# Rotary embedding, interleaved pairs: the first 2 MB loaded in fp32 pieces and stored early in fp32 over SyncE's queue, VectorE by 8 positions

## Chip, cores, metric

One core of a Trainium2 chip. The time is device microseconds of one execution; a profile's span is the part of it between the first and last instruction (316.0 us of a run that took 317.78). All times below are medians of fast runs unless a single profile is named.

## The reference

```python
# x: (8, 2048, 16, 64) fp32 ; cos, sin: (2048, 32) fp32
x1, x2 = x_pairs[..., 0], x_pairs[..., 1]
out1 = x1 * cos - x2 * sin
out2 = x1 * sin + x2 * cos          # out: pairs interleaved again, fp32
```

64 MiB go in, 64 MiB come out; there is little arithmetic per byte.

## The kernel before

A tile holds one batch in bf16: 128 partitions, each with 16 positions of 1024 elements. GpSimd's DMAs cast fp32 to bf16 on the way in and back on the way out; five tile buffers are in use. VectorE rotates in place with three instructions for each group of KP positions. Two things go over SyncE's queue, whose DMAs here do not cast: the first positions of batch 0 (fp32 into a staging buffer, ScalarE casts), and the last positions of batch 7 (ScalarE casts back).

```python
    KP = 4 ; NX = 5 ; HEAD = 2 ; TAIL = 4
    def store(b, k1=K):
        nc.gpsimd.dma_start(out=out_t[b, :, :k1], in_=tiles[b][:, :k1])
    def rotate(b, k0, k1):                     # three TENSOR_TENSOR on positions k0..k1
        ...
        head = stage.tile([P, TAIL, HD], fp32, name="st")
        for k in range(HEAD):
            nc.sync.dma_start(out=head[:, k : k + 1], in_=x_t[0, :, k : k + 1])
        nc.sync.dma_start(out=cos_sb, in_=cos_t)
        nc.sync.dma_start(out=sin_sb, in_=sin_t)
        load(0, HEAD)
        for b in range(1, NX):
            load(b)
        nc.scalar.copy(out=tiles[0][:, :HEAD], in_=head[:, :HEAD])
        # ... cos and sin spread into bf16 tables (VectorE)
        for b in range(B):
            # ... rotate(b, ...) over all positions
            if b < B - 1:
                store(b)
            if b >= 1 and b - 1 + NX < B:
                load(b - 1 + NX)               # waits until store(b - 1) has landed
        store(B - 1, K - TAIL)
        tail = stage.tile([P, TAIL, HD], fp32, name="st")
        nc.scalar.copy(out=tiles[B - 2][:1, 0, :1], in_=tiles[B - 1][:1, K - 1, :1])
        nc.scalar.copy(out=tail, in_=tiles[B - 1][:, K - TAIL :])
        nc.sync.dma_start(out=out_t[B - 1, :, K - TAIL :], in_=tail)
```

## Time and profile before

| | before |
|---|---|
| time, median of 6 runs | 317.45 us (317.34 to 317.79) |
| VectorE busy | 221.8 us (70%) |
| DMA queues' share of 16 engines | 96.8% + 3.1% |
| VectorE starts | 44.2 us |
| batch 1's store issued / its first row on a DMA engine | 102.2 / 120.6 us |

The two DMA queues' shares are to be read as one: together they are 99.9%, so the DMA engines are practically always full. The last row holds the slack: batch 1's store stood in the queue for 18 us before an engine got to it. The lines are in the prediction below.

### The profile page before, as it was taken

The numbers are of one execution on the slowest core, as the hardware profiler recorded it, in microseconds if no ns is written. First come the engines' busy times: TensorE is split into PE (matmuls) and PEld (weight loads), VectorE is DVE, ScalarE is ACT, GpSimd is POOL, SyncE is SP. The second block draws the span as 40 slices with busy tenths as digits, with TensorE's granted clock in tenths as the row PEclk, the third lists the DMA queues.
The fourth block names the chain that finished last, engine by engine and source line by source line (L and its number), as shares of the span: only waits on it lengthen the run. The fifth ranks groups of instructions, "written<-read, shape, count | busy, mean of one in ns | idle before, by whom it ended". The sixth has DMA issues, their size and how long they took to land.

```text
span 316.0 us, 198 instructions
## 1 busy us (share of the span) xinstructions
DVE 221.8 (70%) x102; ACT 6.9 (2%) x4; POOL 8.9 (3%) x20
## 2 busy tenths in 40 slices
DVE  0000039999999999999999999999999999100000
ACT  1200000000000000000000000000000000000400
POOL 3000000000000000000000000000000000000000
DMA  9899999999999999999999999999999999999996
GB/s 241 198 257 212 212 207 236 228 199 199 253 212 265 398 498 431 398 332 261 203 399 465 328 203 199 481 448 265 199 307 423 398 440 481 406 398 481 417 431 263
DMA packets 3025, 101.72 MB, mean 322 GB/s; under 512 B 336, under 2 KB 336, under 8 KB 848
## 3 DMA queue, kind: packets, MB, share of 16 engines
q0 software_dynamic: 2304, 98.04, 96.8%
q1 hardware_dynamic: 720, 3.67, 3.1%
q14 instruction: 1, 0.01, 0.0%
HBM read 67.63 MB, written 67.11 MB: 426 GB/s over the span
## 4 chain that ended last, share of the span: by engine, by line
another core or an unknown queue 91%; DMA 2%; ACTq 1%; ACT 1%; SPq 0%; issue 0%
DMA st<-in_x_dram 2%; ACTq L144 1%; ACT xt L92 1%; ACT L92 0%; SPq L85 0%; ACT xt L116 0%; ACTq L116 0%; ACTq L92 0%
## 5 line engine op out<-in xcount | busy, mean ns | idle before, releaser
L75 DVE TENSOR_TENSOR xt<-xt,c_tab 128x4096 bf16<-128x4096 bf16 (+1 forms) x33 | 73.5, 2228 | 1.1
L80 DVE TENSOR_TENSOR xt<-xt,qt 128x4096 bf16<-128x4096 bf16 (+1 forms) x33 | 73.5, 2228 | 1.1
L74 DVE TENSOR_TENSOR qt<-xt,s_tab 128x4096 bf16<-128x4096 bf16 (+1 forms) x33 | 73.5, 2228 | 1.1
L94 DVE CAST s_tab<-sin_sb 128x512 bf16<-128x512 f32 x1 | 0.5, 453 | 44.2 <-DMA sin_sb<-in_sin_dram 44.2
L59 POOL DMA_DIRECT2D out_dram<-xt x8 | 4.3, 535 | 202.1 <-DVE xt L80 202.1
L116 ACT COPY xt<-xt 1x1 bf16<-1x1 bf16 x1 | 0.2, 193 | 286.3 <-DMA out_dram<-xt 286.3
L56 POOL DMA_DIRECT2D xt<-in_x_dram x8 | 4.4, 561 | 52.1 <-DMA out_dram<-xt 51.3
L117 ACT CAST st<-xt 128x4096 f32<-128x4096 bf16 x1 | 3.6, 3599 | 0.0
L92 ACT CAST xt<-st 128x2048 bf16<-128x2048 f32 x1 | 1.9, 1899 | 0.0
L92 ACT ACT_TABLE_LOAD x1 | 1.3, 1283 | 6.4 <-DMA st<-in_x_dram 6.4
L96 DVE CAST c_tab<-cos_sb 128x1024 bf16<-128x1024 f32 x1 | 0.7, 684 | 0.0
L95 DVE TENSOR_SCALAR s_tab<-sin_sb 128x512 bf16<-128x512 f32 x1 | 0.4, 443 | 0.0
L133 POOL MEMSET const-float32-0.0<- 128x1 f32 x1 | 0.1, 99 | 0.2 <-issue 0.2
L133 POOL MEMSET const-bfloat16-1.0<- 128x1 bf16 x1 | 0.1, 102 | 0.0
L133 POOL MEMSET const-float32-1.0<- 128x1 f32 x1 | 0.1, 99 | 0.0
L133 POOL MEMSET const-uint8-127<- 128x1 uint8 x1 | 0.1, 99 | 0.0
## 6 DMA issues: line engine op xcount, KB each, us to landing
xt<-in_x_dram POOLq DMA_DIRECT2D x7, 4096.0 KB, 58.0
out_dram<-xt POOLq DMA_DIRECT2D x1, 6144.0 KB, 49.4
xt<-in_x_dram POOLq DMA_DIRECT2D x1, 3584.0 KB, 22.7
out_dram<-st SPq DMA_DIRECT2D x1, 2048.0 KB, 15.5
st<-in_x_dram SPq DMA_DIRECT2D x2, 512.0 KB, 4.5
cos_sb<-in_cos_dram SPq DMA_DIRECT2D x1, 256.0 KB, 22.4
sin_sb<-in_sin_dram SPq DMA_DIRECT2D x1, 256.0 KB, 42.1
out_dram<-xt POOLq DMA_DIRECT2D x7, 54.0
```

The source lines that it names most:

```text
L56: nc.gpsimd.dma_start(out=tiles[b][:, k0:], in_=x_t[b, :, k0:])
L59: nc.gpsimd.dma_start(out=out_t[b, :, :k1], in_=tiles[b][:, :k1])
L74: nc.vector.tensor_tensor(out=rows(qt[:, :nk]), in0=rows(xp), in1=tab(s_tab), op=mult)
L75: nc.vector.tensor_tensor(out=rows(xp), in0=rows(xp), in1=tab(c_tab), op=mult)
L80: nc.vector.tensor_tensor(out=x3, in0=x3, in1=q_swap, op=add)
L92: nc.scalar.copy(out=tiles[0][:, :HEAD], in_=head[:, :HEAD])
L94: nc.vector.tensor_copy(out=s2[:, :, 0], in_=sin_sb)
L95: nc.vector.tensor_scalar_mul(s2[:, :, 1], sin_sb, -1.0)
L96: nc.vector.tensor_copy(out=c_tab.rearrange("p k (i j) -> p (k i) j", j=2), in_=cos_sb.to_broadcast([P, K * D2, 2]),)
L117: nc.scalar.copy(out=tail, in_=tiles[B - 1][:, K - TAIL :])
L133: nc = _bacc.Bacc("TRN2", target_bir_lowering=False, num_devices=1)
L144: with _tile.TileContext(nc) as tc:
```

## The change

The intent: start on data that need no casting DMA, let the first part of the result leave while the loads still run, and spare VectorE some fixed costs.

```diff
-    KP = 4
+    KP = 8
-    HEAD = 2
+    HEAD = 4
+    HEAD_RUNS = [(0, 1), (1, 2), (2, 4)]
...
-    def store(b, k1=K):
-        nc.gpsimd.dma_start(out=out_t[b, :, :k1], in_=tiles[b][:, :k1])
+    def store(b, k0=0, k1=K):
+        nc.gpsimd.dma_start(out=out_t[b, :, k0:k1], in_=tiles[b][:, k0:k1])
...
-        head = stage.tile([P, TAIL, HD], fp32, name="st")
-        for k in range(HEAD):
-            nc.sync.dma_start(out=head[:, k : k + 1], in_=x_t[0, :, k : k + 1])
+        head = stage.tile([P, HEAD, HD], fp32, name="st")
+        for k0, k1 in HEAD_RUNS:
+            nc.sync.dma_start(out=head[:, k0:k1], in_=x_t[0, :, k0:k1])
...
                 rotate(b, 0, HEAD)
+                nc.scalar.copy(out=head, in_=tiles[b][:, :HEAD])
+                for k0, k1 in HEAD_RUNS:
+                    nc.sync.dma_start(out=out_t[b, :, k0:k1], in_=head[:, k0:k1])
                 rotate(b, HEAD, KP)
...
-                store(b)
+                store(b, HEAD if b == 0 else 0)
```

More of the change, by code (lines that the diff above doesn't have):

```diff
@@ L90 @@
             load(b)
-        nc.scalar.copy(out=tiles[0][:, :HEAD], in_=head[:, :HEAD])
+        nc.scalar.copy(out=tiles[0][:, :HEAD], in_=head)
         s2 = s_tab.rearrange("p k (i j) -> p (k i) j", j=2)
@@ L106 @@
             if b < B - 1:
-                store(b)
+                store(b, HEAD if b == 0 else 0)
             if b >= 1 and b - 1 + NX < B:
                 load(b - 1 + NX)
-        store(B - 1, K - TAIL)
+        store(B - 1, 0, K - TAIL)
         tail = stage.tile([P, TAIL, HD], fp32, name="st")
```

## The prediction

> **What bounds the kernel now.** The page of the kernel before comes first, its busy shares and slices, because they say which resource has no free time.
>
> ```profile
> DVE 221.8 (70%) x102; ACT 6.9 (2%) x4; POOL 8.9 (3%) x20
> DMA  9899999999999999999999999999999999999996
> GB/s 241 198 257 212 212 207 236 228 199 199 253 212 265 398 498 431 398 332 261 203 399 465 328 203 199 481 448 265 199 307 423 398 440 481 406 398 481 417 431 263
> q0 software_dynamic: 2304, 98.04, 96.8%
> q1 hardware_dynamic: 720, 3.67, 3.1%
> HBM read 67.63 MB, written 67.11 MB: 426 GB/s over the span
> ```
>
> VectorE is busy 70% of the span, the DMA engines practically always: every slice is an 8 or a 9 up to the last. The GB/s row seems to say that stores (about 420) run twice as fast as loads (about 210), but a load is counted by its bf16 bytes in SBUF and a store by its fp32 bytes in HBM. In HBM bytes both are the same. The whole traffic, 67.63 + 67.11 = 134.74 MB, went in 316.0 us, 426 GB/s with both ends of the span included.
>
> Next, the stretches of 5 us around the change from loads to stores:
>
> ```profile
> 90.00:95.00 5.00, 4.90 (x4) 0.00 (x0) 0.00 (x0) 1.00 0.97 210
> 95.00:100.00 5.00, 4.93 (x3) 0.00 (x0) 0.00 (x0) 1.00 1.04 210
> 100.00:105.00 5.00, 4.93 (x3) 0.00 (x0) 0.54 (x1) 1.00 0.98 419
> 105.00:110.00 5.00, 4.93 (x3) 0.00 (x0) 0.00 (x0) 1.00 0.98 419
> ```
>
> The two last columns are DMA share and GB/s: no dip where the five loads end and the first store begins. Then GpSimd's timeline, to see how far ahead of the DMA engines its queue is filled:
>
> ```profile
> 74.53 0.54 POOL L59 DMA_DIRECT2D out_dram<-xt  x1 [70.48 <-DVE xt L80]
> 102.17 0.54 POOL L59 DMA_DIRECT2D out_dram<-xt  x1 [27.11 <-DVE xt L80]
> 121.79 0.54 POOL L56 DMA_DIRECT2D xt<-in_x_dram  x1 [19.08 <-DMA out_dram<-xt]
> 130.09 0.53 POOL L59 DMA_DIRECT2D out_dram<-xt  x1 [7.77 <-DVE xt L80]
> ```
>
> The store of batch 0 is issued at 74.53 us, while by the trace's packet records the fifth load holds the DMA engines until 101; that is 27 us of slack. The store of batch 1 comes at 102.17, and the store of batch 0 lands at 121.79 (the load that waits for it starts then): 19 us of slack. This second slack is the smallest in the kernel, and the number to watch. Two landings that GpSimd waited for, 121.79 and 141.09, are one transfer of 8.39 MB apart: 19.3 us, or 435 GB/s.
>
> Last, what VectorE waited for at the start, and how long the table loads took:
>
> ```profile
> DVE s_tab L94 <- DMA sin_sb<-in_sin_dram: 44.2, 1, 44.2
> cos_sb<-in_cos_dram SPq DMA_DIRECT2D x1, 256.0 KB, 22.4
> sin_sb<-in_sin_dram SPq DMA_DIRECT2D x1, 256.0 KB, 42.1
> ```
>
> 256 KB would take 0.6 us at full rate. In the packet records each DMA engine has 8 rows of each table and 8 rows of each batch; one table row runs after each batch row (64 KB of fp32, 2.43 us). So cos takes as long as the load of batch 0, sin as long as that of batch 1. VectorE idles 44 us, but the DMA engines have loads to do until 101 us, so that costs nothing.
>
> **What the Trainium skill says.** "DMA: Bandwidth & Descriptors", section "Queues, rings and completion order": each DMA engine goes round robin over the queues that have work, a packet at a time. The trace agrees, with one row per turn: 22.4 and 42.1 us for the two tables. The same page, "Where 436 GB/s comes from", puts the ceiling of the fabric at 435 GB/s; the 19.3 us per 8.39 MB above are that. The same page's "Rules for kernel authors" says that spreading DMAs over issuing engines gains no bandwidth; before has both queues together at 99.9%, with a share near 1 whichever runs. "SBUF — State Buffer", section on the "DVE blocks DMA" trap, says that a VectorE instruction in a two-port mode keeps GpSimd from writing descriptors; with queues this full, no wait in this trace shows such a thing, and it bears on rival 2.
>
> **The change, part by part.**
>
> *Bytes.* 1 MB more of x comes, and 2 MB of the result goes, over SP as fp32 instead of over GpSimd with a cast. The HBM bytes stay 134.74 MB, and they set the DMA time. Shorter rows cost a little: 4 KB took 0.159 us where its share of a long row is 2.43/16 = 0.152. Over the two 4 KB pieces of the result (16 rows on each engine) that is 0.1 us; with the 8 KB rows and the shorter rows of batch 0, I allow 0.3 us.
>
> *Start.* The first two pieces are as before. By the packet records they hold all 16 engines from about 3 us until GpSimd's first rows start, at 5.1 to 6.0 us, so there is no hole for the third piece to fill. It stands in SP's order where cos stood, and should be served as cos was: one row after each row of batch 0.
>
> *VectorE's start.* The rows of batch 0's load are now 12 positions, 48 KB, 1.83 us; with one 8 KB row (0.3 us) each, 8 turns are 17 us: third piece in by about 23 us. Then cos beside batch 1, 8 x (2.42 + 0.08) = 20 us: 43. Then sin beside batch 2, 20 us: 63. VectorE starts at about 63.5 us, not 44.2.
>
> *VectorE's pace.* 2048 elements took 1.22 us and 4096 took 2.29, so 1.07 for each 2048 and about 0.16 fixed; 8192 should take 4.43, with the gap 4.47. A batch is then 6 x 4.47 = 26.8 us, before 12 x 2.33 = 28.0. From 63.5: tables 1.3, positions 0 to 3 in 3 x 2.33 = 7.0 (71.8), positions 4 to 7 another 7.0 (78.8), 8 to 15 in 3 x 4.47 = 13.4 (92.2). Batch 1 ends at 92.2 + 26.8 = 119.0. Tile buffers and loads don't hold it: the fifth load is in at about 102.
>
> *Early result.* ScalarE casts 128x4096 in 3.60 us as at the end of the kernel before, 71.8 to 75.5, and SP issues three pieces. Their 24 rows on each engine alternate with batch rows of about 2.4 us, so they would be in flight until some time beyond 115 us; nothing waits for them but the buffer of the tail, at 296 us.
>
> *The queue.* All work that the engines have before batch 1's store, from the first GpSimd row at 5.1 us: load of batch 0, 14.6; third piece 2.4; tables 1.3; four loads 77.4; store of batch 0 without its first 4 positions, 14.6; early result 4.8; in all 115.1 us. The same sum for before is 115.0, and predicts 120.1 where the records show batch 1's store starting at 120.6; so I add 0.5: the engines run dry at 120.7 (first engine) to about 121.6. Batch 0's store is issued at 92.2, ahead of 102: no hole. Batch 1's store is issued at 119.0. Its slack is 2 us where it was 19. How long GpSimd takes from issue to first packet is not bare in this trace: its first load, issued at 1.24, had its first row at 5.14, but behind SP's rows. With 1.5 to 2 us no engine idles, or for half a microsecond; with 3.9 us they idle 2 us. I put 0.5 us as the likely loss.
>
> *After that* slack grows again: batch 2's store comes at about 146 us, and by then the store of batch 1 and the sixth load (39 us of work) are queued. VectorE ends at about 281 us, not 269, but the last store only gets the engines at 294. The end (cast, tail over SP) is not changed.
>
> *Sum.* 317.4 + 0.3 (short rows) + 0.5 (hole at 121 us) = 318.2; with some chance of no loss at all, 318.1 us.
>
> **Rivals.** 1: mixing reads with writes early, or SP's path without a cast, moves more bytes per microsecond. For it: some slices read 498. Against it: these have a share above 1, because their packets are counted where they start, and whole transfers take 19.3 us whether loads or stores; and the SP rows ran no faster than the others. It would make 310 to 314 us. 2: the lost slack becomes a real hole, because VectorE starts later than I think, or because instructions of 4.4 us delay descriptors. Each microsecond beyond 2 is a microsecond of time; 5 us late makes 321. For it: a margin of 2 us out of a sum of 119 is thin. Against it: the SP rows still queued fill the first part of it, and that is already in the sum. 3: the third piece gets through before GpSimd's rows start, as the first two did. Then cos and sin land 20 us earlier, VectorE starts at 44, all slack stays, and the time is 317.4 to 317.7. Against it: cos, in the same place, did not get through. 4: VectorE by 8 positions as a gain. It saves 1.1 us per batch on an engine with idle time: nothing.
>
> **Range and chances.** DMA work cannot shrink, which closes the low end at 317.0. The high end is the hole: 2 us of it, and a little, 320.2. Faster by 2% would need 311 us, less than the bytes take at 435 GB/s (134.74 / 435 = 309.7) with the some 5 us of start and end: 1%. Slower by 2% needs 323.7, a hole of over 5 us: 4%.
>
> **What would show it.** VectorE's wait for sin ends near 63 us; the 8192-element instructions take 4.4 us; GpSimd issues the second store near 119; DMA shares stay near 1 with at most one dip, at 120 to 124 us. If VectorE starts at 44, rival 3 holds; if the DMA row shows several dips or a time above 321, the queue sum is wrong; a time below 316 would mean that the bytes do not set the DMA time.

## More of the kernel before

One more view belongs here, because it turned out to matter: what the trace keeps for the line on which the program ends. SyncE's entries there (number, then duration in ns, first and last start in us) and the issue of the tail's store, with 15.5 us to landing:

```profile
L144 SPq EVENT_SEMAPHORE  x9: 17/28/28, 300.0 to 315.9; - x9
L144 SPq DRAIN  x3: 7/7/7, 315.2 to 315.5; - x3
299.59 0.35 SPq L118 DMA_DIRECT2D out_dram<-st  x1
out_dram<-st SPq DMA_DIRECT2D x1, 2048.0 KB, 15.5
```

The tail (the last positions of batch 7) lands at 299.59 + 15.5 = 315.1 us, SyncE's first DRAIN, with which it ends its program, is at 315.2, and 0.8 us later the span ends.

## The result

| | before | after |
|---|---|---|
| time, median of 6 runs | 317.45 us | 318.18 us (318.07 to 318.25) |
| ratio, with 95% interval | | 1.0021 (1.0008 to 1.0034) |
| VectorE starts | 44.2 us | 63.5 us |
| batch 1's store issued / first row | 102.2 / 120.6 us | 119.2 / 120.6 us |

Ratios are the mean time of one kernel's fast runs over that of the other's of the same rounds, so not quite the ratio of the two medians. The time is the predicted one within 0.1 us, and the difference is small but outside the noise. The page, the waits and GpSimd's timeline of the changed kernel, to be laid beside those in the prediction:

```profile
DVE 214.2 (68%) x54; ACT 12.3 (4%) x5; POOL 8.9 (3%) x20
q0 software_dynamic: 2304, 95.42, 94.2%
q1 hardware_dynamic: 1296, 6.82, 6.3%
HBM read 67.63 MB, written 67.11 MB: 426 GB/s over the span
...
DVE s_tab L97 <- DMA sin_sb<-in_sin_dram: 63.5, 1, 63.5
...
92.42 0.54 POOL L62 DMA_DIRECT2D out_dram<-xt  x1 [88.38 <-DVE xt L83]
119.18 0.54 POOL L62 DMA_DIRECT2D out_dram<-xt  x1 [26.22 <-DVE xt L83]
120.39 0.53 POOL L59 DMA_DIRECT2D xt<-in_x_dram  x1 [0.67 <-DMA out_dram<-xt]
```

The HBM bytes are the same, some of them have gone from queue 0 to queue 1, and VectorE starts one load later. The slack has gone: GpSimd used to wait 19.08 us between the second store and the landing of the first one, and now waits 0.67. Whether that left the DMA engines idle is in the row for 118 to 124 us, cut into 40 slices. A packet is counted in the slice where it starts, so with long rows a full engine shows groups of 9 with zeros between; it is short rows that show a hole. First before, then after:

```profile
DMA  9999900000000000099999000000000099999000
```

```profile
DMA  0082888979797969699999900000000009999990
```

From 118.3 to 120.5 us the changed kernel's row is filled with small packets, SyncE's third piece of the early result; then batch 1's store starts. A count of the packets running at each moment shows 16, one on each engine, from 6 us to 311 us in both kernels. There is no hole.

So where are the 0.7 us? SyncE's entries on the program's last line, after:

```profile
L150 SPq EVENT_SEMAPHORE  x11: 17/28/28, 312.0 to 316.3; - x11
L150 SPq DRAIN  x3: 7/7/7, 315.5 to 315.8; - x3
299.60 0.33 SPq L124 DMA_DIRECT2D out_dram<-st  x1
out_dram<-st SPq DMA_DIRECT2D x1, 2048.0 KB, 15.4
```

The tail lands at 315.0 us, 0.1 us *earlier* than in the profile before, but the first DRAIN is at 315.5. The trace's records of single waits say why. At the end SyncE waits, one after another, on every semaphore that a DMA has used. In the records the 9 DMAs of its own queue use 8 semaphores in turn, so the ninth, the tail's store, shares that of the first load. In the list of waits that semaphore comes second; the 7 waits behind it, each long satisfied, start 61 ns apart and take 0.43 us. In the kernel before, the tail's store was the fifth of 5, and its wait was the last of the list. From last landing to end of span: 0.87 us before, 1.33 after. That is 0.45 of the 0.73 us between the medians.

The other 0.28 us, by subtraction, lie before the last landing, although the two profiles seem to say the opposite. The profile of the kernel before is of a run of 317.78 us, 0.33 above the median; the changed kernel's is of one of 318.12, 0.06 below its median. Two runs below, b_kp8 and a_noearly, take as long as the kernel before, and their profiles are of median runs: by the packet records batch 1's store has its first row at 120.30 and 120.34 us, and the tail lands at 314.92 and 314.90. Against these the changed kernel, with 120.56 and 315.03, is 0.2 us late at batch 1's store and 0.1 at the end.

### The profile page after: what moved, and what is told of

It reads as the page before. It is cut to its first block, busy times and chain, and to the rows that moved or that the text cites. A ratio compares the mean times of both kernels' runs of the same rounds, so it can differ in the third digit from the quotient of the medians.

```text
span 316.4 us, 162 instructions
## 1 busy us (share of the span) xinstructions
DVE 214.2 (68%) x54; ACT 12.3 (4%) x5; POOL 8.9 (3%) x20
## 4 chain that ended last, share of the span: by engine, by line
DVE 34%; issue 25%; another core or an unknown queue 20%; DMA 13%; ACT 1%; POOL 1%; ACTq 0%; POOLq 0%
DMA out_dram<-xt 13%; DVE xt L83 11%; DVE xt L78 11%; DVE qt L77 11%; ACT st L123 1%; POOL out_dram L62 1%; POOL xt L59 0%; DVE s_tab L97 0%; DVE s_tab L98 0%; POOLq L62 0%; DVE c_tab L99 0%; ACT xt L122 0%; ACTq L123 0%; ACTq L122 0%
## 5 line engine op out<-in xcount | busy, mean ns | idle before, releaser
L78 DVE TENSOR_TENSOR xt<-xt,c_tab 128x8192 bf16<-128x8192 bf16 (+1 forms) x17 | 71.0, 4175 | 0.6
L83 DVE TENSOR_TENSOR xt<-xt,qt 128x8192 bf16<-128x8192 bf16 (+1 forms) x17 | 71.0, 4175 | 0.6
L77 DVE TENSOR_TENSOR qt<-xt,s_tab 128x8192 bf16<-128x8192 bf16 (+1 forms) x17 | 71.0, 4174 | 0.5
L97 DVE CAST s_tab<-sin_sb 128x512 bf16<-128x512 f32 x1 | 0.5, 453 | 63.5 <-DMA sin_sb<-in_sin_dram 63.5
L106 ACT CAST st<-xt 128x4096 f32<-128x4096 bf16 x1 | 3.6, 3606 | 43.4 <-DVE xt L83 43.4
L123 ACT CAST st<-xt 128x4096 f32<-128x4096 bf16 x1 | 3.6, 3605 | 0.0
L95 ACT CAST xt<-st 128x4096 bf16<-128x4096 f32 x1 | 3.6, 3604 | 0.0
```

The costliest lines, as they stand in the source:

```text
L77: nc.vector.tensor_tensor(out=rows(qt[:, :nk]), in0=rows(xp), in1=tab(s_tab), op=mult)
L78: nc.vector.tensor_tensor(out=rows(xp), in0=rows(xp), in1=tab(c_tab), op=mult)
L83: nc.vector.tensor_tensor(out=x3, in0=x3, in1=q_swap, op=add)
L95: nc.scalar.copy(out=tiles[0][:, :HEAD], in_=head)
L97: nc.vector.tensor_copy(out=s2[:, :, 0], in_=sin_sb)
L106: nc.scalar.copy(out=head, in_=tiles[b][:, :HEAD])
```

## The experiments

The edits are against the changed kernel unless another is named. "Before" is the kernel before, run on the same chip in the same rounds. "End" is from the last landing to the end of the span, in the profile. Two theories stand: my sum (0.3 us for short rows, 0.5 for a hole), and the end waits. The runs were made on two chips; the kernel before took 317.48 to 317.51 us.

**a_again**: no edit.

> The changed kernel itself, as the reference of this call: 318.1 to 318.3 us, 0.6 to 0.8 us over the kernel before. Theory (end waits): the last DMA lands no later than in the kernel before, and about 0.4 us of the difference lie after that landing, in 7 further waits of SyncE of about 62 ns each. Rival (my sum): the last landing is 0.8 us later, and what follows it is the same.

Measured: 318.18 us, before 317.50, ratio 1.0023 (1.0009 to 1.0036). Last landing 315.01, end 1.33 us. As the first time. The last landing is 0.1 us later than in a_noearly and b_kp8, not 0.8, which speaks for the end waits.

**a_eight**: one DMA fewer.

```diff
-                for k0, k1 in HEAD_RUNS:
+                for k0, k1 in [(0, 2), (2, 4)]:
                     nc.sync.dma_start(out=out_t[b, :, k0:k1], ...
```

> The early result in 2 pieces of 8 KB rows in place of 3, so the kernel has 8 DMAs on SyncE's queue, not 9, and the tail's store does not share a semaphore with the first load. Theory (end waits): the wait for the tail becomes the last of SyncE's list, what follows the last landing drops from 1.3 to about 0.9 us, and the time by 0.4 us to about 317.8. Rival (rows and hole): the 4 KB rows gone save at most 0.1 us, time 318.1.

Measured: 317.88 us (317.66 to 317.95), ratio 1.0012 (0.9999 to 1.0025). SyncE's DRAIN and the tail's store:

```profile
L150 SPq DRAIN  x3: 7/7/7, 315.4 to 315.7; - x3
299.81 0.33 SPq L124 DMA_DIRECT2D out_dram<-st  x1
out_dram<-st SPq DMA_DIRECT2D x1, 2048.0 KB, 15.5
```

End 0.88 us: no wait between the tail's and the DRAIN. The list is as long as in the changed kernel (11 entries), so it is the tail's place in it that counts, not its length. The end moved as foreseen, by 0.45 us; the time by 0.30. The rest went into a later last landing (315.29 us, 0.26 later in this profile, which is of a run 0.07 above the median).

**b_nine**: four idle loads more in the kernel before.

```diff
         nc.sync.dma_start(out=sin_sb, in_=sin_t)
+        for i in range(4):
+            spare = consts.tile([P, 16], fp32, name=f"spare{i}")
+            nc.sync.dma_start(out=spare, in_=sin_t[:, i * 16 : (i + 1) * 16])
```

> The kernel before with 4 tiny loads more (64 bytes a row) on SyncE's queue, 9 in all; nothing reads them. Theory (end waits): the tail's store shares the first load's semaphore, its wait comes early in SyncE's list, and the time rises by 0.4 us to about 317.85 with no later last landing (32 rows of 64 bytes on each DMA engine are at most 0.1 us of DMA time). Rival: 317.4 to 317.5, unchanged.

Measured: 318.41 us (318.22 to 318.64), before 317.50, ratio 1.003 (1.0018 to 1.0043).

```profile
L147 SPq DRAIN  x3: 7/7/7, 316.1 to 316.4; - x3
300.00 0.35 SPq L121 DMA_DIRECT2D out_dram<-st  x1
out_dram<-st SPq DMA_DIRECT2D x1, 2048.0 KB, 15.6
```

End 1.31 us, not 0.87: the other direction of the same effect. The last landing also came 0.4 us later than in the kernel before, where I had foreseen 0.1. My 0.1 was too low: of the 512 small rows 384 are recorded with 24 ns, 64 with 51 and 64 with 2455 (about the time of one long row). At 24 ns, the 32 rows of an engine are some 0.8 us, an estimate from these records; that is enough for the 0.4, but which part of a record holds up other rows isn't shown.

**a_kp4**: VectorE by 4 positions, everything else as changed.

```diff
-    KP = 8
+    KP = 4
...
-                rotate(b, HEAD, KP)
-            for k0 in range(KP if b == 0 else 0, K, KP):
+                rotate(b, HEAD, 8)
+            for k0 in range(8 if b == 0 else 0, K, KP):
```

> The changed kernel with VectorE by 4 positions as before. VectorE then takes 28.0 us for a batch in place of 26.75: batch 1's store should be issued at about 120.9 us and not at 119.2, its first rows come 1.5 us later at 122.4, and the DMA engines run dry at 120.5 to 121.2. Theory (the slack at batch 1's store is used up): a hole of about 1.3 us opens, time 319.4 to 319.6. Rival (VectorE is hidden, as it is busy 68%): 318.2, as the changed kernel.

Measured: 319.34 us (319.19 to 319.39), ratio 1.0058 (1.0045 to 1.007), 1.16 us over the changed kernel and just under the foreseen 319.4. GpSimd's timeline and the DMA row of the same 118 to 124 us:

```profile
120.96 0.54 POOL L62 DMA_DIRECT2D out_dram<-xt  x1 [27.38 <-DVE xt L83]
DMA  0027498999999999945210000009900000000000
```

Now the small packets thin out (4, 5, 2, 1) at 120.6 to 121.1 us and zeros follow, until batch 1's store begins, everywhere at once, at 122.06. The packet records give 1.22 us idle on the mean engine. The store was issued 1.78 us later than in the changed kernel and cost 1.2, so the changed kernel had some 0.6 us of slack left, not 2. And with no row ahead of it, the delay from issue to first row is bare: 122.06 - 120.96 = 1.10 us.

**b_kp8**: the kernel before with KP = 8 alone.

> The kernel before with VectorE by 8 positions alone. VectorE's busy time falls by some 7 us to about 214.5 (fewer fixed costs of 0.16 us), none of it on the path of the DMA engines: 317.3 to 317.6, as the kernel before. Rival (coarser steps delay the first store, or long instructions delay GpSimd's descriptors): over 318.

Measured: 317.56 us (317.35 to 317.99), before 317.51, ratio 1.0004 (0.999 to 1.0018). VectorE is busy 214.2 us, 7.6 less, for nothing. In this kernel the part is worthless, and in the changed one it keeps 1.2 us away (a_kp4).

**a_four**: one SyncE piece more ahead of the tables.

```diff
-        for k0, k1 in HEAD_RUNS:
+        for k0, k1 in [(0, 1), (1, 2), (2, 3), (3, 4)]:
             nc.sync.dma_start(out=head[:, k0:k1], in_=x_t[0, :, k0:k1])
```

> The first 2 MB of x in four pieces of 4 KB rows in place of 4, 4 and 8 KB: one more piece ahead of the tables on SyncE's queue. If each piece takes as long as one batch's load (one row per turn), sin lands at about 82.9 us and not at 63.5. Theory (slack of 2 us): batch 0's store is issued at 112 and batch 1's at 138.5; the DMA engines have nothing to do for about 18 us in two holes, time about 336. Rival (a VectorE start some us later is hidden): under 320.

Measured: 337.30 us (337.15 to 337.48), ratio 1.0624 (1.061 to 1.0639). Waits, and stretches of 10 us with the DMA share in the last but one column:

```profile
83.36 0.45 DVE L97 CAST s_tab<-sin_sb 128x512 bf16<-128x512 f32 x1 [83.36 <-DMA sin_sb<-in_sin_dram]
...
100.00:110.00 10.00, 9.93 (x3) 0.00 (x0) 0.00 (x0) 1.00 0.49 205
110.00:120.00 10.00, 9.93 (x3) 0.00 (x0) 0.54 (x1) 1.00 0.74 315
120.00:130.00 10.00, 9.90 (x4) 0.00 (x0) 0.00 (x0) 1.00 0.74 315
130.00:140.00 10.00, 9.93 (x3) 0.00 (x0) 1.01 (x2) 1.00 0.00 0
```

VectorE starts 19.8 us later than in the changed kernel, and two holes open, 7.0 us before batch 0's store and 12.2 us before batch 1's: 19.2 us idle, 19.1 us of time. Beyond the last half microsecond of slack the path through sin, VectorE and the second store sets the time one to one.

**a_noearly**: no early result.

```diff
-                nc.scalar.copy(out=head, in_=tiles[b][:, :HEAD])
-                for k0, k1 in HEAD_RUNS:
-                    nc.sync.dma_start(out=out_t[b, :, k0:k1], in_=head[:, k0:k1])
...
-                store(b, HEAD if b == 0 else 0)
+                store(b)
```

> The changed kernel without the early fp32 result: batch 0 is stored whole by GpSimd. The bytes are the same and nothing waits for the early result, so the DMA engines run dry at the same moment, about 121 us. Theory: the last landing does not move by more than 0.2 us, the tail's store is the 6th DMA of SyncE's queue, with a semaphore of its own, and its wait is the last of the list: 317.7 us. Rival (the early rows fill a hole): batch 0's store ends 5 us earlier without them, a hole of up to 4 us, time 319 to 322; rival 2 (early stores mix well with loads): slower by up to 1 us.

Measured: 317.53 us (317.44 to 317.67), before 317.51, ratio 1.0002. End 0.86 us, last landing 314.90, no idle engine at 121 us. The head in fp32 pieces with its late start of VectorE costs nothing by itself; all of the 0.7 us come with the early result: the end waits by the three DMAs that it adds, and the rest before the last landing.

**a_one**: the early result in one DMA.

```diff
-                for k0, k1 in HEAD_RUNS:
+                for k0, k1 in [(0, HEAD)]:
                     nc.sync.dma_start(out=out_t[b, :, k0:k1], ...
```

> The early result in one DMA of 16 KB rows, 7 DMAs on SyncE's queue. Theory (end waits and a little for rows): tail's wait last in the list, 0.88 us after the last landing; 317.6 to 317.8, between the kernel without early result (317.53) and that with two pieces (317.88). Rival (the early result costs by its bytes, not by its rows): as with two pieces, 317.9.

Measured: 317.76 us (317.55 to 317.88), ratio 1.0007. End 0.88 us. Without the end waits an early result costs 0.23 us in one piece and 0.35 in two (317.88 less 317.53). The packet records agree: batch 1's store has its first row at 120.55 us here and at 120.68 in a_eight, 120.34 in a_noearly. These differences are hardly larger than the spread of one kernel's runs; whether rows, bytes or completions make them stays open.

**a_acttab**: the tables over ScalarE's queue.

```diff
-        nc.sync.dma_start(out=cos_sb, in_=cos_t)
-        nc.sync.dma_start(out=sin_sb, in_=sin_t)
+        nc.scalar.dma_start(out=cos_sb, in_=cos_t)
+        nc.scalar.dma_start(out=sin_sb, in_=sin_t)
```

> The changed kernel with cos and sin loaded over ScalarE's queue, beside the head pieces and not behind them. Theory: the tables land before 10 us or at worst with the first two batches' loads (44 us), the third piece at about 23; VectorE starts between 28 and 44 us, batch 1's store is issued 20 to 36 us earlier than in the changed kernel, and the time does not fall below 318.0 by more than the end waits allow: no DMA engine was idle at 121 us, so the slack that comes back is worth nothing, 317.7 to 318.3. Rival (the late start costs some of the 0.7 us): 317.5 or less with 10 waits after the last landing.

Measured: 318.20 us (318.01 to 318.42), ratio 1.0023 (1.001 to 1.0037). Batch 1's store is issued at 95.9 us, 23 us sooner than in the changed kernel, and the time is the same to 0.02 us; end 1.32 us. That SyncE's queue has only 7 DMAs here does not shorten the end: in the records the two on ScalarE's queue take their turn among the same 8 semaphores, and the tail's store shares that of cos. The late start costs nothing in the changed kernel, and the slack that comes back is worth nothing but safety. (The start differs too: GpSimd's first row comes at 5.7 us, not 5.2, so a compensation of a few tenths is not excluded.)

**a_tabfirst**: the tables ahead of the head pieces, on SyncE's queue.

```diff
+        nc.sync.dma_start(out=cos_sb, in_=cos_t)
+        nc.sync.dma_start(out=sin_sb, in_=sin_t)
         for k0, k1 in HEAD_RUNS:
             nc.sync.dma_start(out=head[:, k0:k1], in_=x_t[0, :, k0:k1])
-        nc.sync.dma_start(out=cos_sb, in_=cos_t)
-        nc.sync.dma_start(out=sin_sb, in_=sin_t)
```

> The changed kernel with cos and sin ahead of the head pieces on SyncE's queue. VectorE's tables are then ready before 10 us; the pieces come after, one row per turn, so the third piece lands at about 24 to 43 us and VectorE starts on batch 0 then. Theory: 20 us or more of slack come back at batch 1's store, and the time does not fall, 318.0 to 318.3, because no DMA engine was idle there: the 0.7 us don't come from the late start. Rival (a hole at 121 us costs 0.5): 317.6.

Measured: 323.31 us by the fast runs (322.96 to 323.66), ratio 1.0182 (1.0168 to 1.0196), and one run of 340.67, which the profile caught. Both my expectations failed: I had meant to give slack back and took more away.

> One look more at the kernel with the tables first, whose five runs were 323.0 to 323.7 and once 340.7, for a profile of the faster kind. Theory (how many of SyncE's DMAs get all their rows in before GpSimd's first rows decides): in the faster kind the third piece lands one batch load earlier, at about 63 us in place of 82.8, VectorE starts on batch 0 at about 68, batch 1's store is issued at about 123 and the hole is 3 to 5 us. Rival (a slower DMA rate): rows of 64 KB take longer than 2.43 us.

Measured: 323.32 us, a single run, of the faster kind. VectorE's, ScalarE's and GpSimd's timelines of the slower kind, then of the faster:

```profile
19.63 0.45 DVE L97 CAST s_tab<-sin_sb 128x512 bf16<-128x512 f32 x1 [19.63 <-DMA sin_sb<-in_sin_dram]
82.83 1.28 ACT L95 ACT_TABLE_LOAD   x1 [82.83 <-DMA st<-in_x_dram]
142.12 0.54 POOL L62 DMA_DIRECT2D out_dram<-xt  x1 [26.22 <-DVE xt L83]
```

```profile
4.16 0.45 DVE L97 CAST s_tab<-sin_sb 128x512 bf16<-128x512 f32 x1 [4.16 <-DMA sin_sb<-in_sin_dram]
65.47 1.28 ACT L95 ACT_TABLE_LOAD   x1 [65.47 <-DMA st<-in_x_dram]
124.77 0.54 POOL L62 DMA_DIRECT2D out_dram<-xt  x1 [26.22 <-DVE xt L83]
```

The tables are small enough to be gone at 3.4 us, and GpSimd's first row runs then, not at 5.1. In the faster kind all 256 table rows get in before the batch rows, so the three pieces take one load each and the third lands at 65 us. In the slower kind 7 of the 256 rows, all of sin and apparently of one engine, were left: sin waits for batch 0's load (19.6 us), and on that engine all pieces come one load later. VectorE then also waits for ScalarE's table load and cast (4.9 us). The faster kind issues batch 1's store 5.6 us later than the changed kernel, idles 5.15 us and costs 5.1 us more. So this "slow" run is no throttled chip (its clock is 1.0, as in all runs) but, by these two profiles, a race at the start, and it costs 17 us. The long rows take 2.43 us in both kinds; the rival falls.

None of these versions beats the kernel before; a_noearly and b_kp8 equal it.

## Why the prediction was right

Its number was right, 318.1 for 318.18. Its mechanism was right where it placed the time (the bytes set it; the change eats slack and gains nothing). Of the two small terms of its sum one, the hole of 0.5 us, was not there, and a term of 0.45 us, the waits at the end, was missing.

- *What bounds it*: right. The same HBM bytes, and 16 of 16 engines running from 6 to 311 us in both kernels.
- *VectorE's start at 63.5, 8192 elements in 4.43 us, stores at 92.2 and 119.0*: measured 63.5, 4.43, 92.4, 119.2. The rule behind it, one SyncE row per GpSimd row, so one SyncE DMA per load, was tested by a_four: one piece more, 19.8 us later.
- *Batch 1's store has 2 us of slack*: overstated. By a_kp4 0.6 us were left, by a_four 19.8 - 19.2 = 0.6. My moment of running dry, 120.7 to 121.6, was about right (120.6 to 121.4 by the packet records of a_kp4); issue to first row takes 1.1 us, which I had not taken off before I called it slack.
- *A hole of 0.5 us as the likely loss*: the step that failed. The hole is zero, as the same step's other half said (no idle with 1.5 to 2 us of delay; it was 1.1).
- *Short rows, 0.3 us*: right in size, not shown in cause. The early result costs some 0.2 to 0.35 us without end waits, and batch 1's store starts 0.2 us later than in a_noearly. But a_one still costs 0.23 with rows of 16 KB, which in the tail's store took 0.611 us, per byte no more than a long row (2.45 us for 64 KB), so shortness may not be the reason. My check of the queue sum also leaned on one profile, of a run 0.33 us above the median: its 120.6 us for batch 1's store are 120.3 in b_kp8.
- *"The end (cast, tail over SP) is not changed"*: wrong. The cast and the store are the same, but the waits behind them are not: 0.45 us, the larger part of the difference, shown by taking it away (a_eight, a_one, a_noearly: 0.86 to 0.88 us) and by adding it to the kernel before (b_nine: 1.31).
- *Rivals*: 1 falls, the DMA rate did not change. 2 is false here but close: a_kp4 has the hole that was described. 3 falls, sin came at 63.5. 4 was right that the faster VectorE brings nothing to the kernel before (b_kp8), but in the changed kernel it holds off 1.2 us, which I had in the working and did not say.

Two errors, a hole that was not there (0.5 us) and an end that I thought unchanged (0.45 us), had nearly the same size. That the number came out within 0.1 us is therefore luck.

## What to carry to other kernels

When the DMA engines are full from end to end, judge a change by its slack: when is each transfer issued, and when do the engines get to it. A change that only eats slack looks harmless in the time, and the next half microsecond costs fully. A small DMA on a second queue beside long-row DMAs took as long here as a whole long transfer (18 to 20 us for 256 KB to 1 MB), so the order on that queue, and how many small DMAs stand ahead of the one that the compute waits for, mattered more than their bytes. And before explaining a difference of a few tenths of a microsecond by the data path, compare what comes after the last landing, and look how far the two profiled runs are from their medians.

## What the Trainium skill lacked or had wrong

- "DMA: Bandwidth & Descriptors", section "Queues, rings and completion order", says that an engine drains a packet of some 9 to 17 descriptors before it turns to another queue. The trace records one packet for each row and not how many descriptors a row has, so that number is neither confirmed nor refuted. Here the engine turned after one row: a DMA of 8 short rows on each engine took as long as one load (19.8 us for one piece more, a_four). That a small DMA is stretched so by a big one is not said.
- The same section says nothing of who goes first at the start. GpSimd's first row came at 5.1 us behind two fp32 pieces on SyncE's queue, and at 3.4 us behind the two small tables, of which it sometimes cut off a few rows (323.3 or 340.7 us, a_tabfirst).
- "SBUF — State Buffer", section "Who interferes with whom", says that TENSOR_TENSOR did not stall GpSimd's DMAs. The runs agree: 1.10 us from issue to first row in a_kp4 with VectorE busy throughout, and "DMA: Bandwidth & Descriptors", table "Specifications", has about 1 us for it. Nothing to mend.
- "Runtime: NRT & Kernel Launch", section "The ~15µs preamble/postamble breakdown", has a wait for all engines after the kernel as one figure, about 1.5 us. What is seen here stands on the program's own last line, and no run shows whether the page means the same: what follows the last landing was 0.87 or 1.33 us, by the place of the last DMA's semaphore in SyncE's list of waits, 61 ns each. No page that I read has that list.
